# A branch unit behind each half-size product of v and g, the decays' parts between g's products, and three weight blocks multiplied beside x's loads

## The chip, the cores and the metric

The kernel runs on one core of one Trainium2 chip. The metric is the device time of one execution in microseconds. A core has a matrix engine (TensorE, PE in the rows), a vector engine (VectorE, DVE), a scalar engine (ScalarE, ACT), GpSimd (POOL) and SyncE (SP), which here only issues transfers. Each engine works through its own list of instructions in order and waits for the others through semaphores.

## The reference

A decoder trunk of one layer over 512 tokens and 1024 channels, in float32:

```python
h = rms_norm(x, norm_mix[l])
z = h @ w_in[l]
z_rnn, z_q, z_k, z_v, z_g, z_dec, z_mq, z_gate = jnp.split(z, split_idx, axis=-1)
xr = causal_dwconv(z_rnn, rnn_conv_w[l], rnn_conv_b[l])
out_a = rg_lru(xr, rg_w_a[l], rg_b_a[l], rg_w_x[l], rg_b_x[l], rg_lambda[l])
dec_logit = (z_dec @ gla_w_decay[l] + gla_b_decay[l]).astype(jnp.float32)
log_alpha = (jax.nn.log_sigmoid(dec_logit) / GLA_NORMALIZER).reshape(bsz, slen, GLA_HEADS, GLA_DK)
o_gla = chunked_gla(z_q, z_k, z_v, log_alpha)
out_b = rms_norm(o_gla, gla_norm[l]) * jax.nn.silu(z_g)
...
out_c = jnp.einsum("bhsm,bmhd->bshd", prob, mv).reshape(bsz, slen, MIX_WIDTH)
branches = jnp.stack([out_a, out_b, out_c], axis=2)
proj = jnp.einsum("bsnc,ncd->bsnd", branches, w_branch[l])
gates = jax.nn.sigmoid(z_gate).reshape(bsz, slen, N_BRANCHES, D_MODEL)
x = x + jnp.sum(gates * proj, axis=2) @ w_out[l]
```

After it come a gated MLP with a short causal convolution and a final norm, which the change leaves alone.

## The kernel before

**Products.** Each float32 operand is split in two rounded parts (`split`: ScalarE rounds the high part, L97, VectorE subtracts to get the low part, L98), and each product is three matmuls: high by high, high by low, low by high. `mm3` (L104) issues all but the start's.

**Units, steps and lead.** The program is a list (`prog`) of units and steps. A unit multiplies one weight block; its weights are fetched and split two units ahead (`AHEAD`). A gate or input unit (`hold`, `proj_in`) is 24 matmuls of 512 columns, a branch unit (`held`) 18, followed by VectorE's product with the gate (L641) and sum (L642). `weave` spreads steps among units by count; `blend` puts units of a second list among those of a first. Split weights live in three buffers each (`whi`, `wlo`), raw ones in four; SyncE issues the loads in the order in which the program asks for them.

**The start.** `start` multiplies two 1024 x 128 blocks of the input weights (raw query weights, `wch`) while x's eight row blocks still arrive; the products (L419) go two row blocks at a time. Further blocks follow as units (`qu`).

**Half-size products.** The products for v (`v_fast`, 400 columns with the low-rank decay columns) and g (`g_fast`, 384 columns) go by halves of tokens and channels in seven products instead of eight (`seven`): a1, a2, c1, c2, b1, b2, b3, each of two parts (p0, p1) of 12 matmuls. They share two banks of sums: after a1, a2, c1, ... the sum so far is read (`v_read`: L812 and L815 by ScalarE for a1 and a2, L821 and L824 by VectorE), and the next product is added to the same bank, so it has to wait for the read. c1, c2, b1 and b2 multiply sums of the normed activations (`h_sum1`, `h_sum4`, `h_quarter`), which VectorE adds and which are split like weights (`h_ready`). Some weights are sums too: GpSimd's transfers add a second block to one already loaded (L299).

**Around them.** `blend` puts four gate units (g0[0:4]) and three branch units (p0[0:3]) among the 28 parts of v and g. `lru_out` splits the recurrence's outputs (oa), which the branch units multiply. `decay_weights` loads the low-rank decay weights: a memset by GpSimd, three transfers by SyncE (L869), the rounding by ScalarE (L871) and VectorE (L873). `decay_in` transposes z_dec (L878, L880); `decay_logit` multiplies (L894) and takes Abs (L897) and the minimum with zero (L898); `decay_log` takes Exp (L904) and Ln (L907) of all four heads; `decay_sum` sums along the tokens; these ran beside the gate units g0[4:]. `decay_apply` (L928 to L939) with the branch units p0[3:], then `k_end` (transposes, L946), `intra`, `state`, `gla_out`, `gla_norm`, `gla_flip` and `silu` with the second branch's gate units g1, one list of steps for each.

## Time and profile before

| | before |
|---|---|
| median of 3 runs | 941.22 us (940.19 to 942.44) |
| the profiled execution | 941.12 us |
| its span, first to last instruction | 939.4 us |
| TensorE busy | 921.3 us, 98% |
| VectorE busy | 636.6 us, 68% |
| ScalarE busy | 488.2 us, 52% |

The profile is of one execution; the times in its rows count from the span's start. The instructions of TensorE overlap, so the length of one row (0.39 us for 512 columns) is not what it adds to the time: that is the distance from its start to the next one's.

### The profile page before, as it was taken

The numbers are of one execution on the slowest core, as the hardware profiler recorded it, in microseconds if no ns is written. First come the engines' busy times: TensorE is split into PE (matmuls) and PEld (weight loads), VectorE is DVE, ScalarE is ACT, GpSimd is POOL, SyncE is SP. The second block draws the span as 40 slices with busy tenths as digits, with TensorE's granted clock in tenths as the row PEclk, the third lists the DMA queues.
The fourth block names the chain that finished last, engine by engine and source line by source line (L and its number), as shares of the span: only waits on it lengthen the run. The fifth ranks groups of instructions, "written<-read, shape, count | busy, mean of one in ns | idle before, by whom it ended". The sixth has DMA issues, their size and how long they took to land.

```text
span 939.4 us, 11996 instructions
## 1 busy us (share of the span) xinstructions
PE 921.3 (98%) x4390; PEld 779.7 (83%) x4390; DVE 636.6 (68%) x1117; ACT 488.2 (52%) x796; POOL 90.9 (10%) x133
## 2 busy tenths in 40 slices
PE   9999999999998999999999999999999999999996
PEld 7899888888877998878888898888888888888885
DVE  6996745565788454795767665555686666698765
ACT  6765555685845345864434424344345444545544
POOL 0000000000053141000000000000010130012102
PEclk9999999999999999999999999999999999999999
DMA  7435223213369594231146401233364685357612
GB/s 250 160 119 196 88 80 108 85 59 106 111 161 186 130 202 135 76 119 51 51 135 225 167 23 45 92 111 112 135 114 138 146 227 119 110 126 184 162 45 89
DMA packets 45562, 116.93 MB, mean 124 GB/s; under 512 B 5520, under 2 KB 12864, under 8 KB 45504
## 3 DMA queue, kind: packets, MB, share of 16 engines
q1 hardware_dynamic: 33152, 94.28, 30.3%
q0 software_dynamic: 11776, 20.85, 13.0%
q10 hardware_dynamic: 576, 1.05, 0.3%
q8 instruction: 34, 0.56, 0.2%
q14 instruction: 24, 0.20, 0.1%
HBM read 111.69 MB, written 3.67 MB: 123 GB/s over the span
## 4 chain that ended last, share of the span: by engine, by line
PE 88%; DVE 6%; ACT 3%; issue 1%; DMA 1%; POOL 0%; SPq 0%; DVEq 0%; ACTq 0%
PE mm L104 81%; PE sm L104 2%; PE mm L419 1%; DVE wlo L98 1%; PE sm L983 1%; DMA m<-in_xT 1%; DVE f L920 0%; PE sm L969 0%; PE sm L604 0%; PE sm L985 0%; PE sm L585 0%; DVE f L774 0%; DMA f<-in_wdecay 0%; DVE r L98 0%; PE sm L956 0%
## 5 line engine op out<-in xcount | busy, mean ns | idle before, releaser
L98 DVE TENSOR_TENSOR wlo<-raw,whi 128x1024 fp32r<-128x1024 f32 (+2 forms) x155 | 172.4, 1115 | 161.0 <-PE mm L104 75.7
L97 ACT ACTIVATE whi<-raw 128x1024 fp32r<-128x1024 f32 (+2 forms) x155 | 149.7, 970 | 173.2 <-PE mm L104 159.5
L104 PE MATMUL mm<-whi,r 128*128 128x512 f32 (+2 forms) x568 | 172.7, 374 | 3.5 <-ACT r L97 1.8
L104 PE MATMUL mm<-h2l,whi 128*128 128x512 f32 x360 | 140.1, 389 | 0.0
L104 PE MATMUL mm<-h2h,whi 128*128 128x512 f32 x360 | 139.9, 389 | 0.0
L104 PEld LDWEIGHTS mm<-whi,r 128*128 128x128 f32 x568 | 106.4, 189 | 19.3 <-DVE r L98 2.3
L104 PE MATMUL mm<-hh,whi 128*128 128x512 f32 x288 | 113.8, 395 | 2.3 <-ACT whi L97 2.3
L104 PE MATMUL mm<-hl,whi 128*128 128x512 f32 x288 | 113.0, 392 | 0.0
L104 PE MATMUL mm<-wlo,r 128*128 128x512 f32 (+2 forms) x284 | 106.2, 374 | 0.4 <-DVE wlo L98 0.4
L104 PE MATMUL mm<-r,whi 128*128 128x512 f32 (+1 forms) x448 | 98.9, 369 | 0.0
L104 PEld LDWEIGHTS mm<-r,whi 128*128 128x128 f32 x448 | 77.8, 189 | 14.1 <-DVE r L98 0.2
L104 PE MATMUL mm<-h2h,wlo 128*128 128x512 f32 x360 | 88.9, 389 | 0.0
L97 ACT ACTIVATE whi<-f 128x512 fp32r<-128x512 f32 (+2 forms) x90 | 48.3, 581 | 74.6 <-PE mm L104 64.5
L104 PEld LDWEIGHTS mm<-h2h,wlo 128*128 128x128 f32 x360 | 67.6, 188 | 14.0
L104 PEld LDWEIGHTS mm<-h2l,whi 128*128 128x128 f32 x360 | 67.6, 188 | 14.0
L104 PEld LDWEIGHTS mm<-h2h,whi 128*128 128x128 f32 x360 | 67.5, 188 | 14.0
L98 DVE TENSOR_TENSOR wlo<-f,whi 128x512 fp32r<-128x512 f32 (+2 forms) x90 | 53.7, 631 | 35.8 <-ACT whi L97 19.6
L299 POOL DMA_DIRECT2D f<-in_wdown x40 | 35.1, 986 | 438.9 <-DVE wlo L98 415.8
L1127 DVE SCALAR_TENSOR_TENSOR f<-mm,prm,f 128x511 f32<-128x511 f32 x96 | 71.4, 745 | 6.9 <-ACT f L1125 6.1
L104 PE MATMUL mm<-hh,wlo 128*128 128x512 f32 x288 | 71.2, 389 | 0.0
L104 PEld LDWEIGHTS mm<-hh,whi 128*128 128x128 f32 x288 | 54.1, 188 | 13.9 <-ACT whi L97 3.0
L104 PEld LDWEIGHTS mm<-hh,wlo 128*128 128x128 f32 x288 | 54.1, 188 | 11.3
(243 smaller groups left out, 1313.2 us busy)
## 6 DMA issues: line engine op xcount, KB each, us to landing
raw<-in_wup SPq DMA_DIRECT2D x48, 512.0 KB, 3.6
raw<-in_wch SPq DMA_DIRECT2D x40, 512.0 KB, 3.6
f<-in_wdown POOLq DMA_DIRECT2D x40, 256.0 KB, 5.3
raw<-in_wbr SPq DMA_DIRECT2D x24, 384.0 KB, 3.1
raw<-in_wdown SPq DMA_DIRECT2D x14, 512.0 KB, 3.7
f<-in_wdown SPq DMA_DIRECT2D x20, 256.0 KB, 4.3
raw<-in_wout SPq DMA_DIRECT2D x8, 512.0 KB, 3.4
f<-in_wv POOLq DMA_DIRECT2D x16, 200.0 KB, 5.6
```

The lines of the kernel that those rows point to most:

```text
L97: nc.scalar.activation(hi, src, AF.Copy)
L98: (eng or nc.vector).tensor_tensor(out=lo, in0=src, in1=hi.bitcast(F32), op=ALU.subtract)
L104: nc.tensor.matmul(ps, lhsT=l, rhs=r, start=first and i == 0, stop=last and i == len(seq) - 1, skip_group_check=more)
L299: nc.gpsimd.dma_start(raw[to, p][j], src(q, p)[:, j, :], accum_op=ALU.add)
L419: nc.tensor.matmul(ps[u], lhsT=a, rhs=b, start=q == 0 and i in (0, 2), stop=q == KD - 2 and i >= len(seq) - 2)
L983: nc.tensor.matmul(ps[:, j, :], lhsT=sT[h][:, t, :], rhs=vt[t][hp][:, j, :], start=True, stop=t == 0)
L1127: nc.vector.scalar_tensor_tensor(out=a[:, j:], in0=ps[:, :S - j], scalar=col(C_FCW + 48 * (2 - j) + f), in1=a[:, j:], op0=ALU.mult, op1=AL ...
```

## The change

1. `start` multiplies three weight blocks instead of two, one row block of x at a time. The third block's split goes to ordinary slots instead of the `whi` and `wlo` buffers. SyncE's list gets the third block's four pieces in among x's.
2. `lru_rate`'s instructions are issued behind an `lru_split`, not in the start.
3. `run` replaces `blend`: it goes through lists written out by hand. In v_fast the order is a1, g0[0], g0[1], a2, c1, p0[0], g0[2], c2, b1, p0[1], b2, g0[3], b3, with `lru_out` in two groups; before, it was g0[0], a1, g0[1], a2, c1, c2, p0[0], b1, g0[2] and so on. Within the lists a scheduler may weave neighbours.
4. In g_fast come p0[2], `decay_in` and two `decay_logit`, g0[4], the other `decay_logit` and `decay_log`, p0[3], two `decay_sum`, g0[5], two `decay_sum`. g0[6] and g0[7] follow without them.
5. `decay_apply` goes with p0[4:] and g1[0:2], and the steps from `k_end` to the flips with g1[2:], six units instead of eight. g1[0] and g1[1] copy their sums first and take the sigmoid in place at the end (`late_gate`).
6. `h_sum1` is asked for eight units ahead instead of seven.

ScalarE in the value product, where the decay weights are rounded. Before (`mm_2571` and `mm_2578` are a1's banks, `mm_2556` that of g0[0]):

```order
L97 ACTIVATE whi_2616<-raw_2614 128x1024
L871 ACTIVATE r_2513<-f_2508 80x384
L1026 ACTIVATE f_2556<-mm_2531 128x512
L97 ACTIVATE whi_2636<-f_2278 128x400
L97 ACTIVATE whi_2636<-f_2279 128x400
L812 ACTIVATE f_2604<-mm_2571 128x400
L812 ACTIVATE f_2612<-mm_2578 128x400
L97 ACTIVATE r_2642<-f_2460 128x512
```

and now (`mm_2542` and `mm_2549` are a1's banks, `mm_2591` is g0[0]'s, `whi_2632` g0[1]'s weights, `whi_2655` c1's first):

```order
L97 ACTIVATE whi_2632<-raw_2630 128x1024
L97 ACTIVATE whi_2655<-f_2240 128x400
L97 ACTIVATE whi_2655<-f_2241 128x400
L889 ACTIVATE r_2529<-f_2524 80x384
L830 ACTIVATE f_2570<-mm_2542 128x400
L830 ACTIVATE f_2578<-mm_2549 128x400
L1044 ACTIVATE f_2616<-mm_2591 128x512
L97 ACTIVATE r_2618<-f_2177 128x512
```

The rounding of the decay weights stands in both ahead of the reads of a1's banks; before, g0[0]'s read and c1's weight split (which waits for g0[1]'s matmuls) stood between, now c1's weight split stands ahead of it and the reads follow at once.

SyncE's list around the decay weights. Before (`raw_2614` holds g0[1]'s weights, `raw_2646` and `raw_2696` c2's):

```order
L166 DMA raw_2614<-in_wch 128x1024
L303 DMA raw_2646<-in_wv 128x800
L303 DMA raw_2696<-in_wv 128x800
L869 DMA f_2508<-in_wdecay 16x384 x3
L166 DMA raw_2779<-in_wbr 128x768
L166 DMA raw_2922<-in_wch 128x1024
```

and now (`raw_2742` holds p0[0]'s weights, `raw_2748` c2's second part, `raw_2827` those of g0[2]):

```order
L303 DMA raw_2748<-in_wv 128x800
L166 DMA raw_2827<-in_wch 128x1024
L887 DMA f_2524<-in_wdecay 16x384 x3
L294 DMA f_2699<-in_wv 128x400
L294 DMA f_2700<-in_wv 128x400
```

The three transfers of the decay weights have moved behind the loads of p0[0] and g0[2].

ScalarE in g_fast, at the end of c2 and in b1. Now (`whi_3376` holds b1's second part in two halves, `whi_3400` p0[3]'s weights; L915 is Abs, L922 Exp, L925 Ln):

```order
L915 ACTIVATE f_3340<-sm_3338,prm 96x512
L97 ACTIVATE whi_3376<-f_2999 128x384
L915 ACTIVATE f_3346<-sm_3344,prm 96x512
L922 ACT_TABLE_LOAD
L922 ACTIVATE f_3340<-f_3340 96x512
L922 ACTIVATE f_3346<-f_3346 96x512
L925 ACT_TABLE_LOAD
L925 ACTIVATE f_3197<-f_3197 96x512
L925 ACTIVATE f_3203<-f_3203 96x512
L925 ACTIVATE f_3340<-f_3340 96x512
L925 ACTIVATE f_3346<-f_3346 96x512
L97 ACTIVATE whi_3376<-f_3000 128x384
```

Before, the Ln stood beside g0[4:], with only gate units' reads (L1026) and branch weights around:

```order
L1026 ACT_TABLE_LOAD
L1026 ACTIVATE f_3563<-mm_3538 128x512
L907 ACT_TABLE_LOAD
L907 ACTIVATE f_3477<-f_3477 96x512
L907 ACTIVATE f_3516<-f_3516 96x512
L907 ACTIVATE f_3522<-f_3522 96x512
L907 ACTIVATE f_3528<-f_3528 96x512
L1026 ACT_TABLE_LOAD
L1026 ACTIVATE f_3607<-mm_3582 128x512
L97 ACTIVATE whi_3620<-raw_3618 128x768
```

The Exp and Ln of all heads and their table loads now stand between the two halves of the weight split for b1's second part.

```diff
@@ -95,7 +95,7 @@
     def split(hi, lo, src, eng=None):
 
         nc.scalar.activation(hi, src, AF.Copy)
-        (eng or nc.vector).tensor_tensor(out=lo, in0=src, in1=hi.bitcast(F32), op=ALU.subtract)
+        return (eng or nc.vector).tensor_tensor(out=lo, in0=src, in1=hi.bitcast(F32), op=ALU.subtract)
 
     def mm3(ps, terms, first=True, last=True, more=False):
 
@@ -341,6 +341,15 @@
                            lambda key=key, p=p: run(key, p)))
         return us
 
+    def run(*parts):
+
+        for p in parts:
+            if isinstance(p, tuple):
+                unit(*p)
+            else:
+                for v in p:
+                    made_unit(*v) if isinstance(v, tuple) else step(v)
+
     def blend(us, fast, steps=()):
 
         for i, u in enumerate(us):
@@ -396,40 +405,45 @@
 
     def start():
 
-        raw = [wpool.tile([P, D], F32, tag="raw", name=nm("raw"), bufs=NRAW) for _ in range(2)]
-        whi, wlo = ([wpool.tile([P, D], F32R, tag=t, name=nm(t)) for _ in range(2)] for t in ("whi", "wlo"))
-        w = lambda a, u, k, n=1: a[u][:, k * P:(k + n) * P]
+
+        n = 3
+        raw = [wpool.tile([P, D], F32, tag="raw", name=nm("raw"), bufs=NRAW) for _ in range(n)]
+        whi, wlo = ([[wpool.tile([P, D], F32R, tag=t, name=nm(t))] for _ in range(2)] + [[rslot(), rslot()]]
+                    for t in ("whi", "wlo"))
+
+        def w(a, u, k, m=1):
+            j, k = divmod(k, KD // len(a[u]))
+            return a[u][j][:, k * P:(k + m) * P]
+
         for k in range(0, KD, 2):
             nc.sync.dma_start(xs["T"][k], xT[:, k, :])
-            for u in range(2):
-                nc.sync.dma_start(w(raw, u, k, 2), wch[u][:, k * P:(k + 2) * P])
+            for u in range(n):
+                nc.sync.dma_start(raw[u][:, k * P:(k + 2) * P], wch[u][:, k * P:(k + 2) * P])
             nc.sync.dma_start(xs["T"][k + 1], xT[:, k + 1, :])
             if k == 0:
                 nc.sync.dma_start(prm[:, KD:], par[:, KD:])
         for k in range(0, KD, 2):
             x_split([k])
-            for u in range(2):
-                split(w(whi, u, k, 2), w(wlo, u, k, 2), w(raw, u, k, 2))
+            for u in range(n):
+                split(w(whi, u, k, 2), w(wlo, u, k, 2), raw[u][:, k * P:(k + 2) * P])
             x_split([k + 1])
-        ps = [bank(), bank()]
-        for q in range(0, KD, 2):
-            seq = [(w(whi, u, k), xs["r"][k][j], u) for k in (q, q + 1) for u in range(2) for j in range(2)]
-            seq += [(w(wlo, u, k), xs["r"][k][0], u) for k in (q, q + 1) for u in range(2)]
-            for i, (a, b, u) in enumerate(seq):
-                nc.tensor.matmul(ps[u], lhsT=a, rhs=b, start=q == 0 and i in (0, 2),
-                                 stop=q == KD - 2 and i >= len(seq) - 2)
+        ps = [bank() for _ in range(n)]
+        for k in range(KD):
+            seq = [(whi, u, j) for j in range(2) for u in range(n)] + [(wlo, u, 0) for u in range(n)]
+            for i, (a, u, j) in enumerate(seq):
+                nc.tensor.matmul(ps[u], lhsT=w(a, u, k), rhs=xs["r"][k][j], start=k == 0 and i < n,
+                                 stop=k == KD - 1 and i >= len(seq) - n)
         x_squares(range(4))
         for p in ps:
             queries(p)
 
     step(start)
-    qu = [(wch[i], D, lambda w: queries(channel_major(w, KD, lambda k: xs["r"][k]))) for i in range(2, NM)]
+    qu = [(wch[i], D, lambda w: queries(channel_major(w, KD, lambda k: xs["r"][k]))) for i in range(3, NM)]
     xn = [lambda k=k: x_norm(k) for k in range(KD)]
-    weave(qu[:1], [])
     behind[0] = [lambda: x_squares(range(4, KD))]
-    weave(qu[1:2], [x_rstd])
-    weave(qu[2:3], [lambda: mem_load(1), x_bcast])
-    weave(qu[3:], xn[:2])
+    weave(qu[:1], [x_rstd])
+    weave(qu[1:2], [lambda: mem_load(1), x_bcast])
+    weave(qu[2:], xn[:2])
 
 
 
@@ -513,7 +527,7 @@
         return token_units(wmv[pr], 2 * DV, lambda k, t: tuple(mT[k][:, j, t * P:(t + 1) * P] for j in range(2)),
                            NMT, evac)
 
-    behind[2] = [lambda: mem_load(0)]
+    behind[1] = [lambda: mem_load(0)]
     vu = value_units(0) + value_units(1)
     step(mem_rstd)
     ku = [key_unit(i) for i in range(NM)]
@@ -650,6 +664,10 @@
     lsc, nsc = const.tile([P, NB], F32, name="lsc"), const.tile([P, NB], F32, name="nsc")
 
     def lru_rate():
+        with tc.issue_after(lru["split"].ins):
+            lru_rates()
+
+    def lru_rates():
 
         lam = prm[:, C_LAM:C_LAM + NB]
         lt, e, s1, q = stat(NB), stat(NB), stat(NB), stat(NB)
@@ -673,7 +691,7 @@
 
     def lru_split(b):
         lru["x", b] = (rslot((DK, S)), rslot((DK, S)))
-        split(*lru["x", b], xr[b])
+        lru["split"] = split(*lru["x", b], xr[b])
 
     def lru_weights(g):
         return wrg[g], 8 * DK, lambda w: lru.__setitem__(("w", g), w), 2
@@ -853,7 +871,7 @@
 
     def v_fast():
         pre = {k: [(2, lambda p, k=k: h_ready(k, p))] for k in ("c1", "c2", "b1", "b2")}
-        pre["c1"].append((7, h_sum1))
+        pre["c1"].append((8, h_sum1))
         pre["c2"].append((7, h_sum4))
         return seven(lambda q, p: wv[p, int(q[1]) - 1, int(q[2]) - 1], HP + LOW, 2, h_lhs,
                      pre, v_read, 4)
@@ -1020,31 +1038,37 @@
     step(decay_weights)
     gates = {}
 
-    def hold(n, d):
+    def hold(n, d, fn=AF.Sigmoid):
         def evac(ps):
             gates[n, d] = fslot()
-            nc.scalar.activation(gates[n, d], ps, AF.Sigmoid)
+            nc.scalar.activation(gates[n, d], ps, fn)
         return proj_in(18 + 8 * n + d, evac)
+
+    def late_gate(n, d):
+        nc.scalar.activation(gates[n, d], gates[n, d], AF.Sigmoid)
 
     def held(n, acts, d):
         return wbr[n, d], MIX, lambda w: branch(n, acts, d, gates.pop((n, d)))[1][2](w)
 
     g0, p0 = [hold(0, d) for d in range(KD)], [held(0, oa, d) for d in range(KD)]
-    g1 = [hold(1, d) for d in range(KD)]
-    tiles, heads = range(NT), range(H)
-    blend(g0[:2] + p0[:1] + g0[2:3] + p0[1:3] + g0[3:4], v_fast() + g_fast(), each(lru_out, range(NM)) + [lambda: None] * 15)
-
-    weave(g0[4:], [decay_in] + each(decay_logit, heads) + [decay_log] + each(decay_sum, heads))
-    weave(p0[3:], [qk_back] + each(decay_apply, heads))
-    for u, steps in zip(g1, (
-            each(k_end, tiles),
-            each(intra, heads) + [lambda t=t: silu(t, 0) for t in tiles],
-            [lambda n=n, hp=hp: state(n, hp) for n in range(2) for hp in range(2)],
-            [lambda t=t: silu(t, 1) for t in tiles] + [lambda hp=hp: state(2, hp) for hp in range(2)] +
-            [lambda t=t: gla_out(t, 0) for t in range(2)],
-            [lambda t=t: gla_out(t, 0) for t in range(2, 4)] + [lambda t=t: gla_out(t, 1) for t in range(2)],
-            [lambda: gla_norm(0)] + [lambda t=t: gla_out(t, 1) for t in range(2, 4)],
-            each(gla_flip, range(3)) + [lambda: gla_norm(1)],
+    g1 = [hold(1, d, AF.Copy if d < 2 else AF.Sigmoid) for d in range(KD)]
+    tiles, heads, vf, gf = range(NT), range(H), v_fast(), g_fast()
+
+    run(vf[:2], g0[0], each(lru_out, range(3)), vf[2:4], g0[1], each(lru_out, range(3, NM)), vf[4:6], p0[0],
+        vf[6:8], g0[2], vf[8:10], p0[1], vf[10:12], g0[3], vf[12:])
+    run(gf[:2], p0[2], [decay_in] + each(decay_logit, range(2)), gf[2:6], g0[4],
+        each(decay_logit, range(2, H)) + [decay_log], gf[6:10], p0[3], each(decay_sum, range(2)),
+        gf[10:12], g0[5], each(decay_sum, range(2, H)), gf[12:])
+
+    run(g0[6], g0[7], [qk_back])
+    weave(p0[4:] + g1[:2], each(decay_apply, heads))
+    for u, steps in zip(g1[2:], (
+            each(k_end, tiles) + each(intra, heads),
+            [lambda n=n, hp=hp: state(n, hp) for n in range(2) for hp in range(2)] +
+            [lambda t=t: silu(t, 0) for t in tiles],
+            [lambda hp=hp: state(2, hp) for hp in range(2)] + [lambda t=t: gla_out(t, 0) for t in tiles],
+            [lambda: gla_norm(0)] + [lambda t=t: silu(t, 1) for t in tiles] + [lambda t=t: gla_out(t, 1) for t in tiles],
+            each(gla_flip, range(3)) + [lambda: gla_norm(1)] + [lambda d=d: late_gate(1, d) for d in range(2)],
             each(gla_flip, range(3, 6)))):
         weave([u], steps)
     weave([held(1, ob, d) for d in range(KD)], [])
```

## Rows read from the trace of the kernel before

**Rows 1.** Busy time (share of the span) and instructions of an engine, from part 1 of the page.

```profile
PE 921.3 (98%) x4390; PEld 779.7 (83%) x4390; DVE 636.6 (68%) x1117; ACT 488.2 (52%) x796; POOL 90.9 (10%) x133
```

**Rows 2.** The chain of waits that ended last, part 4 of the page: shares by engine, then by engine and line (the row is long; its head is what counts).

```profile
PE 88%; DVE 6%; ACT 3%; issue 1%; DMA 1%; POOL 0%; SPq 0%; DVEq 0%; ACTq 0%
PE mm L104 81%; PE sm L104 2%; PE mm L419 1%; DVE wlo L98 1%; PE sm L983 1%; DMA m<-in_xT 1%; DVE f L920 0%; PE sm L969 0%; PE sm L604 0%; PE sm L985 0%; PE sm L585 0%; DVE f L774 0%; DMA f<-in_wdecay 0%; DVE r L98 0%; PE sm L956 0%
```

**Rows 3.** Two stretches of the start. Columns: from and to; length; busy us (and instructions) of TensorE, of its weight loads, of VectorE, ScalarE and GpSimd; granted clock; share of the DMA engines; GB/s.

```profile
5.00:13.40 8.40, 7.71 (x18) 4.93 (x18) 6.29 (x19) 6.11 (x15) 0.00 (x0) 1.00 0.91 302
13.40:20.90 7.50, 7.50 (x35) 6.16 (x34) 7.16 (x19) 5.00 (x10) 0.00 (x0) 1.00 0.82 303
```

**Rows 4.** The timeline of the start, TensorE and then ScalarE: start, length, engine, line, operation, out<-in, shape, how many, and in brackets the idle time before it and what ended it. `m` is x's transposed row block.

```profile
6.35 1.65 PE L419 MATMUL mm<-r,whi 128*128 128x512 f32 x3 [0.16 <-ACT whi L97]
8.47 2.07 PE L419 MATMUL mm<-r,whi 128*128 128x512 f32 x4 [0.47 <-ACT r L362]
...
5.88 0.42 ACT L97 ACTIVATE whi<-raw 128x256 fp32r<-128x256 f32 x1 [0.54 <-DMA raw<-in_wch]
7.70 0.72 ACT L362 ACTIVATE r<-m,prm 128x512 fp32r<-128x512 f32 x1 [1.40 <-DMA m<-in_xT]
```

**Rows 5.** The timeline of TensorE from the first gate unit (g0[0]) to g0[2], and after the first row the last of the 16 whi matmuls of that unit, the first of a1 and the 22nd of a1.

```profile
257.96 0.39 PE L104 MATMUL mm<-hh,whi 128*128 128x512 f32 x1
...
261.36 0.39 PE L104 MATMUL mm<-hl,whi 128*128 128x512 f32 x1
...
263.40 0.34 PE L104 MATMUL mm<-whi,hh 128*128 128x400 f32 x1
...
267.22 0.34 PE L104 MATMUL mm<-wlo,hh 128*128 128x400 f32 x1
...
269.07 0.50 PE L104 MATMUL mm<-hh,whi 128*128 128x512 f32 x1 [1.15 <-ACT whi L97]
...
281.32 0.81 PE L104 MATMUL mm<-whi,r 128*128 128x400 f32 x3 [0.75 <-DVE r L98]
...
285.04 0.45 PE L104 MATMUL mm<-whi,r 128*128 128x400 f32 x1 [1.78 <-ACT r L97]
...
286.99 1.37 PE L104 MATMUL mm<-whi,r 128*128 128x400 f32 x3 [0.95 <-DVE r L98]
...
304.26 0.50 PE L104 MATMUL mm<-hh,whi 128*128 128x512 f32 x1 [1.15 <-ACT whi L97]
```

**Rows 6.** Stretches of the value product; columns as in rows 3.

```profile
258.00:304.30 46.30, 40.16 (x190) 35.03 (x188) 40.55 (x70) 22.69 (x40) 20.45 (x29) 0.96 0.80 176
280.00:286.40 6.40, 3.39 (x15) 2.47 (x15) 6.40 (x17) 4.85 (x9) 6.34 (x8) 1.00 0.90 129
286.40:290.00 3.60, 3.01 (x9) 2.99 (x10) 2.22 (x4) 0.11 (x1) 0.00 (x0) 0.53 1.02 211
```

**Rows 7.** The timeline of ScalarE in the value product, and the split of a 768-column weight tile from a later place. L871 rounds the decay weights, L1026 reads a gate unit's bank, L812 (two instructions) the two banks of a1.

```profile
267.96 1.06 ACT L97 ACTIVATE whi<-raw 128x1024 fp32r<-128x1024 f32 x1 [1.31 <-PE mm L104]
271.25 0.53 ACT L871 ACTIVATE r<-f 80x384 fp32r<-80x384 f32 x1 [2.23 <-DMA f<-in_wdecay]
271.68 0.58 ACT L1026 ACTIVATE f<-mm 128x512 f32<-128x512 f32 x1
...
273.95 0.88 ACT L812 ACTIVATE f<-mm 128x400 f32<-128x400 f32 x2
...
279.64 0.62 ACT L97 ACTIVATE r<-f 128x512 fp32r<-128x512 f32 x1
...
318.77 0.85 ACT L97 ACTIVATE whi<-raw 128x768 fp32r<-128x768 f32 x1 [1.24 <-PE mm L104]
```

**Rows 8.** The decay weights' transfers by their source line: duration of an issue, first and last start; then the time from issue to landing.

```profile
L869 SPq DMA_DIRECT2D f<-in_wdecay x3: 326/411/412, 266.6 to 267.5; - x3
...
DMA to landing us min/median/max: 2.6/3.7/3.8
```

**Rows 9.** The low half of a 1024-column weight tile on VectorE, in the timeline of VectorE.

```profile
269.05 1.23 DVE L98 TENSOR_TENSOR wlo<-raw,whi 128x1024 fp32r<-128x1024 f32 x1 [0.55 <-ACT whi L97]
```

**Rows 10.** The timeline of ScalarE beside g0[4:]: L897 is Abs, L904 Exp, L907 Ln, L1026 a gate unit's sigmoid.

```profile
370.13 0.69 ACT L897 ACTIVATE f<-sm,prm 96x512 f32<-96x512 f32 x1 [1.48 <-PE sm L894]
370.83 1.28 ACT L904 ACT_TABLE_LOAD   x1
...
379.13 0.67 ACT L897 ACTIVATE f<-sm,prm 96x512 f32<-96x512 f32 x1
379.70 1.15 ACT L904 ACTIVATE f<-f 96x512 f32<-96x512 f32 x2
...
382.76 1.28 ACT L907 ACT_TABLE_LOAD   x1
384.06 2.20 ACT L907 ACTIVATE f<-f 96x512 f32<-96x512 f32 x4
```

**Rows 11.** k_end's first transposes in the timeline of TensorE, and the multiplication that they wait for in that of VectorE.

```profile
415.47 0.47 PE L946 MATMUL sm<-ident,f 96*128 96x96 f32 x3 [1.64 <-DVE f L934]
...
414.74 0.68 DVE L934 TENSOR_TENSOR f<-f,f 96x512 f32<-96x512 f32 x1
```

**Rows 12.** Stretches of decay_apply and of what follows it until the flips; columns as in rows 3.

```profile
390.00:420.00 30.00, 28.36 (x137) 23.26 (x136) 29.57 (x47) 19.66 (x29) 1.99 (x4) 1.00 0.32 108
420.00:464.00 44.00, 44.00 (x232) 38.56 (x231) 28.22 (x74) 19.99 (x53) 0.00 (x0) 1.00 0.18 56
```

## The prediction

> **What bounds the kernel now.** The page's busy times come first: TensorE works through 98% of the span, VectorE 68%, ScalarE 52% [rows 1]. The chain that ended last says the same, 88% of it TensorE [rows 2]. The change keeps every product (the matmuls have the same shapes and the same number), so TensorE's work is a floor, and what can be won is the time in which TensorE stands or runs slowly. I looked for it first in the start, then in TensorE's waits by time, and read the other engines only around those places. Four places matter.
>
> *The start.* From 5.0 to 13.4 us TensorE was given 18 matmuls of 512 columns, from 13.4 to 20.9 us 35 [rows 3]: about 0.43 us each against 0.21 (0.227 in the steady stretch, below). The granted-clock column reads 1.00 for both, so the pace, not that column, tells the slow stretch. Two waits lie in it, 0.16 us for the second weight block's high part and 0.47 us for x's second row block, whose split began when its transfer landed at 7.70 [rows 4].
>
> *The stretch of the value product* (v_fast with the first gates and branch units). A 512-column matmul takes (261.36 − 257.96)/15 = 0.227 us, a 400-column one (267.22 − 263.40)/21 = 0.182 us [rows 5]. Between 257.96 and 304.26 stand two gate units (48 × 0.227 = 10.9), one branch unit (18 × 0.227 = 4.1), four pairs of the seven products (96 × 0.182 = 17.5), one more pair (4.4) and two transposes (0.4): 37.2 us of work in 46.3 us. 9.1 us are lost: 1.15 us each at 269.07 and 304.26, where a gate unit waits for ScalarE's weight split into a buffer that the matmuls just before it had held; waits of 0.75, 1.78 and 0.95 us at 281.32, 285.04 and 286.99, where c1's and c2's activations are late [rows 5], because VectorE was busy for all of 280.0 to 286.4 [rows 6]; and the stretch from 286.4 to 290.0, where the granted clock was 0.53 [rows 6], near the lower of its two levels (1.2 of 2.4 GHz), after these waits.
>
> *k_end* waits 1.64 us for VectorE at 415.47, because decay_apply's last multiplications for head 3 start only at 414.74 [rows 11]; VectorE was busy 29.57 of 30 us there [rows 12].
>
> *The rest* runs without a wait worth counting.
>
> **The change, part by part.**
>
> *Three blocks in the start: −1.5 us.* Nine matmuls now follow each row block of x instead of six, so x's transfers are waited for less; 4 × 128 KB more are fetched in the start, 0.52 MB at 302 GB/s [rows 3] = 1.7 us, which the third block's own load had to move anyway. At the slow pace the first nine matmuls take 9 × 0.43 = 3.8 us, from 5.4 to 9.3, and x's second block is then there (8.47 before [rows 4], plus one more piece of 128 KB, 0.43 us), so the 0.47 us wait goes. Bound one: the fast pace begins at 13.4 as before. Then 18 of the 72 matmuls are done and 54 × 0.227 = 12.3 us follow, to 25.7; before, the 48 matmuls and the third block's 24 ended at 20.9 + 24 × 0.227 = 26.3. Gain 0.6. Bound two: the fast pace comes earlier by the 4 us in which TensorE now works without a gap; each us saves 1 − 0.21/0.43 = 0.5 us, so the gain is 0.6 + 2 = 2.6. I take the middle, 1.5. lru_rate's 18 short VectorE instructions go to a stretch where VectorE is not full: nothing.
>
> *The order of the value stretch: −3.9 us.* The order is now a1, g0[0], g0[1], a2, then c1, p0[0], c2 and g0[2] woven. What goes: both 1.15 us waits, because the buffer that g0[1] splits into was freed by a1, one whole unit (5.4 us) earlier, against 1.06 us for a split [rows 7]. What comes: the decay weights. Their three transfers were issued at 266.6 to 267.5 and landed 3.7 us later [rows 8]; only then could ScalarE round them (L871, 271.25 [rows 7]). In SyncE's order they now stand behind a weight load that waits for g0[1]'s low half. That split runs when g0[0] is done: 257.96 + 4.4 + 5.4 = 267.8, plus 1.23 us on VectorE [rows 9] = 269.1. The load itself and three issues of 0.41 us [rows 8] follow, the last starts at 270.4, landing 274.1. On ScalarE the rounding (0.5) stands ahead of the two reads of a1's banks (0.44 each [rows 7]), and a2, which adds to these banks, must wait for them: it starts at 275.1 instead of 273.2 (267.8 + 5.4). **New wait 1.9 us**; before, those reads had 3 us to spare. Next, p0[0]'s weight split (0.85) now stands ahead of c1's activation split (0.62 [rows 7]) on ScalarE and can start only when a2 is done: c1 waits about 1.5 us. Then VectorE, which waited for the decay weights too and still has 40.55 us of work in these 46.3 [rows 6] (four more splits come in, two go), is late for four low halves in c1 and p0[0]; by counting its list at 0.60 us an instruction I get 0.4, 0.5, 0.8 and 0.15, so 1.85. New waits 1.9 + 1.5 + 1.85 = 5.2, against 9.1 lost before: gain 3.9. Bounds: none of the new waits occurs and 9.1 are won; or the clock falls again as in 286.4 to 290.0 and the waits after it double: nothing is won.
>
> The Trainium skill ("TensorE: Matmul & The Clock Gate", table of its opening section) says that ScalarE and VectorE take their instructions strictly in order. This speaks against the change, and the rows agree: L1026's read of g0[0] at 271.68 follows straight behind L871, which had waited 2.23 us for its transfer [rows 7].
>
> *The decays' parts between g_fast's products: +3.1 us.* Before, decay_in to decay_sum ran beside g0[4:], without a wait of TensorE. Now ScalarE has, between the two halves of the weight split for b1's second part: an Abs (0.57, from 379.13 to 379.70), a table load (1.28), two Exp (1.15), a second load (1.28) and four Ln (2.20) [rows 10]. Counting from the start of g0[4]: TensorE needs 5.4 (unit) + 0.5 (two decay products) + 40 matmuls of 384 columns at 0.175 (0.182 × 384/400) = 12.9 us until it wants the second half. ScalarE's first half waits for the buffer that c2's first part frees at 8.0; after it 8.0 + 0.5 + 0.57 + 1.28 + 1.15 + 1.28 + 2.20 + 0.5 = 15.5. **New wait 2.6 us**, and p0[3]'s weight split behind it (0.85) comes 0.5 us after TensorE has done the two matmuls that stand ahead: 3.1. Bounds 0 (if the buffer's release lets the first half go earlier) and 4. The same four Ln beside g0[4:] cost nothing before, so nothing is won back there.
>
> The Trainium skill ("ScalarE: Activation LUTs", What ACT_TABLE_LOAD costs) puts a switch at 1.28 us of load and 1.38 us of drain. By that, the two loads here would cost 2.8 us more and this term would be 5.9. The trace disagrees: the load at 370.83 starts 0.01 us after the Abs of 370.13 has ended, and the load at 382.76 is followed by the first Ln at 384.06, 0.02 us after its end [rows 10], so no drain is seen.
>
> *decay_apply and k_end: −1.5 us.* decay_apply now runs beside four branch units and two gate units, (4 × 18 + 2 × 24) × 0.227 = 27.3 us, and k_end comes two gate units later, so the 1.64 us wait goes. The rest (k_end to the flips) has six gate units instead of eight: VectorE's 28.22 us of 44 [rows 12] less two weight splits (2.4) in 33 us and the small matmuls. That fits; one place is tight, the last gla_out, whose bank is read behind the first norm's chain: 0.2. The four added table loads of this part fall where ScalarE has 10 us in 30 free [rows 12]: nothing.
>
> **Sum.** −1.5 − 3.9 + 3.1 − 1.5 = −3.8 us. The profiled execution took 941.12 us with a span of 939.4; the median of the runs is 941.22, so I go from there: **937.4 us**.
>
> **Rivals.**
> 1. *All waits vanish.* The decay weights land in time or the order on ScalarE leaves slack: −1.5 − 9.1 − 1.5 and 0 to 1 for the decays, about 930 us. For it: all four places have a wait by name. Against it: both of the queues that I counted are in order.
> 2. *The gains are given back.* The half clock returns after a2's or the decays' wait (286.4 to 290.0 shows it after 3.5 us of waits within 6 us [rows 5, 6]) at some 2 us, and the start gives 0.6: −3.8 + 2 + 0.9, about 940.3, no measurable change. By the drain of the Trainium skill's ScalarE page ("ScalarE: Activation LUTs") the sum would come to 941.2 − 3.8 + 2.8 = 940.2.
> 3. *Slower: one late transfer holds two queues.* ScalarE and VectorE both have an instruction on the decay weights' transfer in front of everything that c1 and p0[0] need. If it lands 2 us later than I put it (its 3.7 us is a median under 0.8 DMA load [rows 6, 8]), every wait of that stretch grows by it: 1.9 + 2, 1.5 + 2, 1.85 + 2, with the half clock's 2: 13.2 lost instead of 9.1, and −1.5 + 4.1 + 3.1 − 1.5 = +4.2 in all, 945 us. It decides from about 11 us lost in the stretch on. Against it: VectorE's backlog cannot grow by more than the delay once.
> 4. *The order doesn't matter*: TensorE's waits only move, 941.
>
> **Chances.** Forecast 0.48, rival 1 0.17, rival 2 with 4 0.22, rival 3 0.13. 0.2% is 1.9 us, about what a measurement of this kernel can tell from no change. The forecast's own range is 935 to 940, of which a tenth is within 0.2%. Faster 0.48 × 0.9 + 0.17 = 0.60, same 0.05 + 0.20 = 0.25, slower 0.13 + 0.02 = 0.15. The range goes from 931, most of rival 1's, to 942.5.
>
> **What would show it.** Start: the 72 matmuls end at 24 to 25.7. Value stretch: no wait of g0[1] or g0[2]; a2 waits about 1.9 us for ScalarE's read of a bank behind the decay weights' rounding; c1 waits for its activation's split. g_fast: b1's second part waits 2 to 3 us for a weight split behind four Ln. k_end without a wait. I am wrong if a2 starts at once, if the Ln row ends before TensorE comes to b1, or if a stretch at the lower clock stands where there was none.

## The result, and the profile after

| | before | after |
|---|---|---|
| median (20 runs each, side by side) | 939.30 us (936.78 to 942.44) | 942.30 us (940.74 to 944.52) |
| ratio | | 1.0034, 95% interval 1.0025 to 1.0042 |
| profiled execution / its span | 941.12 / 939.4 us | 942.34 / 940.5 us |

The change makes the kernel 3.0 us slower. The forecast was 937.4 us, with 942.5 as the upper end. It was reckoned from 941.22, the median of three executions of the kernel before; the median of the twenty is 939.30. So the forecast was 3.8 us less, and 3.0 us more were measured. Of the executions in the section below, one, of the run "Ln later", took 1548.85 us at a mean granted clock of 0.557 and is left out of that run's ratio.

TensorE's waits in the profile after (line of the waiting matmul, engine and line waited for; us in total, times, longest). L830 reads a1's and a2's banks, L495 is VectorE's read of a key bank:

```profile
PE mm L104 <- ACT f L830: 3.1, 1, 3.1
PE mm L104 <- ACT whi L97: 2.7, 1, 2.7
PE mm L104 <- ACT r L97: 1.6, 2, 1.5
...
PE mm L104 <- DVE r L98: 0.8, 2, 0.6
PE mm L104 <- DVE f L495: 0.6, 1, 0.6
PE mm L104 <- DVE wlo L98: 0.6, 1, 0.6
```

The 1.15 us waits for g0[1]'s and g0[2]'s weight splits and the 1.64 us of k_end are gone [rows 5, 11]. Two new ones stand at the top, of 3.1 and 2.7 us. The timeline of TensorE has them (start, length, ..., in brackets the idle time and what ended it):

```profile
274.42 0.45 PE L104 MATMUL mm<-whi,hh 128*128 128x400 f32 x1 [3.12 <-ACT f L830]
...
282.06 0.45 PE L104 MATMUL mm<-whi,r 128*128 128x400 f32 x1 [1.45 <-ACT r L97]
...
290.48 1.10 PE L104 MATMUL mm<-r,whi 128*128 128x512 f32 x3 [0.61 <-DVE r L98]
...
358.71 0.61 PE L104 MATMUL mm<-whi,r 128*128 128x384 f32 x2 [2.71 <-ACT whi L97]
...
360.76 0.69 PE L104 MATMUL mm<-wlo,r 128*128 128x384 f32 x1 [0.58 <-DVE wlo L98]
```

The first row is a2, the second c1, the third the branch unit p0[0], the last two b1's second part of g. Behind both long waits the granted clock was at its lower level (windows; columns as in rows 3, the clock stands third from the end):

```profile
5.00:13.40 8.40, 8.12 (x35) 6.17 (x35) 6.80 (x14) 6.79 (x17) 0.00 (x0) 1.00 1.01 350
13.40:20.90 7.50, 7.50 (x35) 6.22 (x34) 6.42 (x10) 5.57 (x11) 0.00 (x0) 1.00 0.85 313
274.50:278.40 3.90, 3.90 (x13) 3.87 (x14) 3.89 (x8) 1.84 (x5) 0.00 (x0) 0.57 0.63 92
...
360.40:363.80 3.40, 3.04 (x9) 2.85 (x10) 3.29 (x7) 0.71 (x2) 1.31 (x2) 0.50 0.27 41
```

The first of these waits is followed by 0.50 from 275.0 on, the second from 360.4 to 363.8. In the start, TensorE now does 35 matmuls in the window in which it did 18 [rows 3], and the 72 of the three blocks end at 22.4 us.

To see where the time lies, I took the distance from each matmul's start to the next, less the median distance of its shape in the same trace, and summed this over stretches. What comes out is the time lost to waits and to slow matmuls together, in us (good to some 0.3 us in a stretch, since a median that is 1 ns off counts once for every matmul of its shape):

| stretch of the span | 0–20 | 20–120 | 260–320 | 340–380 | 400–420 | 420–460 | whole |
|---|---|---|---|---|---|---|---|
| before | 6.9 | 1.3 | 8.6 | 0.2 | 2.1 | 0.4 | 20.4 |
| after | 3.0 | 3.0 | 8.7 | 5.7 | 0.0 | 1.1 | 22.5 |

The value stretch (260–320) won nothing in these two executions, the decays between g's products (340–380) cost 5.5, k_end's wait is gone, and the start's gain of 3.9 is followed by a loss of 1.7. The profiled execution of before was 1.8 us above the median of its runs (941.12 against 939.30), that of after was at its median; so the two profiles alone show less than the 3.0 us, and the first question is whether the start's 3.9 belong to the kernel or to the execution.

### The profile page after: what moved, and what is told of

Read it like the earlier page. It is cut to its first block, busy times and chain, and to the rows that moved or that the text cites. A ratio compares the mean times of both kernels' runs of the same rounds, so it can differ in the third digit from the quotient of the medians.

```text
span 940.5 us, 12015 instructions
## 1 busy us (share of the span) xinstructions
PE 920.6 (98%) x4390; PEld 779.5 (83%) x4390; DVE 637.3 (68%) x1120; ACT 493.6 (52%) x805; POOL 91.2 (10%) x133
## 4 chain that ended last, share of the span: by engine, by line
PE 92%; DVE 3%; ACT 2%; issue 1%; DMA 1%; POOL 0%; SPq 0%; DVEq 0%; ACTq 0%
PE mm L104 85%; PE mm L434 2%; PE sm L104 2%; DVE wlo L98 1%; DMA f<-in_wdecay 0%; PE sm L987 0%; DMA raw<-in_wch 0%; PE sm L974 0%; PE sm L1001 0%; ACT whi L97 0%; PE sm L618 0%; PE sm L599 0%; PE sm L1134 0%; DVE r L98 0%; DVE m L391 0%
## 5 line engine op out<-in xcount | busy, mean ns | idle before, releaser
L98 DVE TENSOR_TENSOR wlo<-raw,whi 128x1024 fp32r<-128x1024 f32 (+3 forms) x154 | 170.3, 1111 | 152.9 <-PE mm L104 72.6
L97 ACT ACTIVATE whi<-raw 128x1024 fp32r<-128x1024 f32 (+3 forms) x154 | 148.7, 970 | 177.2 <-PE mm L104 153.6
L104 PE MATMUL mm<-r,whi 128*128 128x512 f32 (+1 forms) x432 | 96.3, 370 | 1.7 <-DVE r L98 0.8
L104 PEld LDWEIGHTS mm<-r,whi 128*128 128x128 f32 x432 | 75.3, 190 | 16.3 <-DVE r L98 1.7
```

The source lines that it names most:

```text
L97: nc.scalar.activation(hi, src, AF.Copy)
L98: return (eng or nc.vector).tensor_tensor(out=lo, in0=src, in1=hi.bitcast(F32), op=ALU.subtract)
L104: nc.tensor.matmul(ps, lhsT=l, rhs=r, start=first and i == 0, stop=last and i == len(seq) - 1, skip_group_check=more)
```

## The experiments

The theories, in pairs. On the start: A, its gain is as large as the profiles show; B, it is a matter of the one execution that was profiled. On a2's wait: C, the transfer of the decay weights ahead of the reads of a1's banks causes it and the slow stretch behind it; D, the engines' own work would hold a2 there too. On b1's wait: E, Exp, Ln and their table loads ahead of the weight split cause it; F, g's weights come late by themselves. Each run was timed beside the kernel before, with 4 to 12 executions of its own; the median of the kernel before was 939.65 to 939.79 us there. Gains against the changed kernel ("after") are differences of the two ratios to the kernel before.

**The start alone.** Before, with the three-block start and its lists, without the move of lru_rate:

```diff
-        raw = [... for _ in range(2)]
+        n = 3
+        raw = [... for _ in range(n)]
...
-    behind[2] = [lambda: mem_load(0)]
+    behind[1] = [lambda: mem_load(0)]
```

> The kernel before with the three-block start alone. Theory A (the start really gives what the two profiles show, 26.3 to 22.4 us at the end of the third block, and the loss lies elsewhere): 939.3 - 3.9 = 935.4 us. Rival B (the slow first 8 us of the profile before were the chance of that one execution, since 20 runs of the kernel before spread over 5.7 us): within 1 us of the kernel before, 938.5 to 939.5.

Measured: 938.87 us, ratio 0.9995 (0.9984 to 1.0006). This is what theory B forecast.

**The changed kernel with the old start.**

> The changed kernel with the two-block start of before. Theory A: the start's gain is lost, 942.3 + 3.9 = 946.2 us. Rival B: no change by it, 942 to 943. In both the waits at a2 and in b1 of g stay (3.1 and 2.7 us).

Measured: 941.78 us, ratio 1.0029 (1.0017 to 1.0040), against 1.0034 with the new start. Theory B's number again. This edit leaves `lru_rate` behind the `lru_split`, where the change had put it. The profiles of all kernels with either start say why. The time lost in the first 20 us was 6.9, 4.6, 5.4, 4.7 and 4.5 us in the five with the old start (the kernel before had the largest loss), and 3.0, 3.2, 5.0 and four times 3.3 in the seven with the new one: 5.2 against 3.5 in the mean, a gain of 1.7. From 20 to 120 us it was 1.2 to 1.3 with the old start and 3.0 to 3.1 with the new one: 1.8 given back. The largest piece of that is this wait, in the profile after:

```profile
57.30 1.93 PE L104 MATMUL mm<-r,whi 128*128 128x256 f32 x14 [0.63 <-DVE f L495]
```

The key units need banks that VectorE reads (L495) behind x's and the memory's norms; as I read it, the 24 matmuls drawn into the start are one unit less to cover these norms. That the old start doesn't have the loss is shown, this reason for it is not.

**Only the decay weights' transfers earlier.** The changed kernel; the memset and the three transfers are asked for some 50 us earlier, the rounding stays in its place:

```diff
+    step(lambda: decay_loads())
     weave(b2[8:12], [s for p in zip(each(lru_scan, lo), each(lru_gates, hi)) for s in p])
...
-    def decay_weights():
-        wy = fslot((KZ, H, DK))
+    def decay_loads():
+        wy = gla["wy0"] = fslot((KZ, H, DK))
         nc.gpsimd.memset(wy, 0.0)
         for c in range(0, KZ, 2 * LOW):
             nc.sync.dma_start(wy[c:c + LOW], wdecay)
+    def decay_weights():
+        wy = gla.pop("wy0")
         r = gla["wy"] = rslot((KZ, H, DK))
```

> The changed kernel with only the decay weights' memset and three transfers put earlier (in the recurrence's branch units); their rounding stays where it was. In the run before this one the rounding had been moved too, and VectorE's list with it. Theory C (the transfer in front of the reads of a1's banks is the whole of a2's wait): a2 has no wait, the stretch at 0.50 behind it is gone or stands elsewhere, and 942.3 - 3.1 - 1.7 = 937.5 us. Rival D (the engines' work is the bound there): the 3.1 us come back as waits for VectorE in c1 and p0[0], 941.5 to 942.5 us.

Measured: 936.69 us, ratio 0.9976 (0.9966 to 0.9987), 5.4 us better than after. This is theory C. The time lost in 260–320 fell from 8.7 to 2.3. These are the only waits of TensorE left there, and the granted clock was at its upper level throughout:

```profile
278.24 1.36 PE L104 MATMUL mm<-whi,r 128*128 128x400 f32 x6 [0.39 <-DVE r L98]
...
284.52 1.10 PE L104 MATMUL mm<-r,whi 128*128 128x512 f32 x3 [0.61 <-DVE r L98]
```

What the wait was made of, in the profile after: ScalarE's rounding (L889) and the bank reads (L830), SyncE's issues, and the transfers' landing; then the landing with the early loads:

```profile
273.46 0.52 ACT L889 ACTIVATE r<-f 80x384 fp32r<-80x384 f32 x1 [2.97 <-DMA f<-in_wdecay]
273.89 0.87 ACT L830 ACTIVATE f<-mm 128x400 f32<-128x400 f32 x2
...
265.12 0.33 SPq L166 DMA_DIRECT2D raw<-in_wbr  x1
266.03 0.33 SPq L303 DMA_DIRECT2D raw<-in_wv  x1
267.20 0.33 SPq L166 DMA_DIRECT2D raw<-in_wch  x1
267.62 1.58 SPq L887 DMA_DIRECT2D f<-in_wdecay  x3
...
DMA to landing us min/median/max: 4.7/5.1/5.3
```

```profile
L888 SPq DMA_DIRECT2D f<-in_wdecay x3: 382/412/413, 215.5 to 216.4; - x3
...
DMA to landing us min/median/max: 2.7/3.0/3.2
```

The three small transfers took 5.1 us from issue to landing, behind loads of 384, 400 and 512 KB issued within 2.1 us; 50 us earlier, behind a single load of 512 KB, they took 3.0. That the other loads are what held them was not tried apart. Had they landed in 3.7 us as before [rows 8], a2's wait would be some 1.7 us (an estimate: 3.12 less 1.4).

**The whole decay-weights step earlier,** rounding included, ahead of `lru_decay(1)`.

> The changed kernel with the decay weights loaded and rounded before the last branch units of the recurrence instead of in the value product; nothing else asked for. Theory C (a2 waits because ScalarE stands at the decay weights' transfer, and the clock's lower level follows from that wait): a2's wait of 3.1 us goes, with it the stretch at 0.50 after 275.0 (some 1.7 us): 942.3 - 4.8 = 937.5 us. Rival D (VectorE's and ScalarE's work in the value product is the bound, the transfer only the place where it shows): c1 and p0[0] then wait longer by about what a2 waited, 941.5 to 942.5 us.

Measured: 941.32 us, ratio 1.0021 (1.0010 to 1.0033). Not a clean test. a2's wait went, but the rounding now stood ahead of the recurrence's Exp and Tanh on ScalarE, VectorE's last scan of the recurrence began at 268.2 instead of 263.0, and g0[1]'s low weight half came late:

```profile
268.28 2.67 PE L104 MATMUL mm<-hh,wlo 128*128 128x512 f32 x8 [2.00 <-DVE wlo L98]
```

The granted clock was at 0.50 from 269.6 to 273.0. Some 2 of the 5.2 us by which the scan is later belong to the profiled execution, not to the edit: at 944.00 us it was the longest of the twelve, and its start lost 5.0 us instead of 3.0. Moving the transfers alone was worth 5.4 us; with the rounding moved too, 1.2 are left, which the two intervals hardly tell from nothing.

**The early transfers in the kernel before.** The same edit, old order.

> The kernel before with one edit: the memset and the three transfers of the decay weights are asked for some 50 us earlier, the rounding stays where it was. It asks what the new order of the value stretch adds. Theory G (the order is worth its gain once the transfer is early): in the old order the two waits of 1.15 us for a weight split and c1's and c2's late activations are there all the same, only ScalarE's 2.23 us wait for the transfer goes; the time stays within 2 us of before, 938 to 940 us. Theory H (the transfer was the cause in the old order too: VectorE, busy through 280 to 286.4, had lost its lead in waiting for it): the waits of 0.75, 1.78 and 0.95 us and the stretch at the lower clock at 286.4 go with it, 3.5 + 1.8 = 5.3 us, 934.5 us, as much as the early loads gave the changed kernel, and the new order adds nothing to it.

Measured: 938.05 us, ratio 0.9984 (0.9973 to 0.9996). Nearer to G. The old order keeps its waits:

```profile
266.62 0.50 PE L104 MATMUL mm<-hh,whi 128*128 128x512 f32 x1 [1.15 <-ACT whi L97]
...
280.61 0.45 PE L104 MATMUL mm<-whi,r 128*128 128x400 f32 x1 [1.35 <-ACT r L97]
...
282.81 0.82 PE L104 MATMUL mm<-whi,r 128*128 128x400 f32 x3 [0.85 <-DVE r L98]
...
285.15 0.74 PE L104 MATMUL mm<-r,whi 128*128 128x512 f32 x2 [0.98 <-ACT whi L97]
...
299.62 0.50 PE L104 MATMUL mm<-hh,whi 128*128 128x512 f32 x1 [1.15 <-ACT whi L97]
```

They add up to 5.5 us, where before had 5.8 [rows 5]. What went in this profile is the stretch at the lower clock [rows 6]: 6.7 us lost instead of 8.6. The clock stood at 1.00 where the kernel before had 0.53:

```profile
286.40:290.00 3.60, 3.60 (x22) 3.60 (x21) 1.56 (x4) 0.96 (x2) 0.40 (x1) 1.00 1.10 291
```

This execution took 936.40 us, near the shortest of its twelve. Eight of them, at a mean granted clock of 0.997 or 0.998, took 936.3 to 938.7 us; the four at 0.993 to 0.996 took 939.7 to 940.6, so the stretch was probably not gone from those four (they were not profiled). In these profiles the new order alone wins nothing (8.7), the early transfers alone 1.9 (1.5 by the ratio of the runs), and both together 6.3 (8.6 to 2.3).

**Ln later.** The changed kernel with `decay_log` behind p0[3] and the sums behind it:

```diff
-        each(decay_logit, range(2, H)) + [decay_log], gf[6:10], p0[3], each(decay_sum, range(2)),
-        gf[10:12], g0[5], each(decay_sum, range(2, H)), gf[12:])
+        each(decay_logit, range(2, H)), gf[6:10], p0[3], [decay_log], gf[10:12], each(decay_sum, range(2)), g0[5],
+        gf[12:], each(decay_sum, range(2, H)))
```

> The changed kernel with decay_log asked for behind p0[3] and the decay_sum steps behind b2, so that ScalarE splits the second half of b1's weights and p0[3]'s weights ahead of the Ln and its table load. The gate units stay between g's products. Theory E (ScalarE's order is what costs): b1's wait of 2.7 us, 1.0 us behind it and the stretch at 0.50 go: 942.3 - 5.4 = 936.9 us. Rival F (g's weights come late by themselves): a wait of 1 us or more stays at b1 or moves to the next unit, 939.5 to 940.5 us.

Measured: 935.82 us, ratio 0.9966 (0.9952 to 0.9979). This is theory E: the loss in 340–380 fell from 5.7 to 0.3. ScalarE in the profile after, then with this edit (L922 Exp, L925 Ln):

```profile
351.61 0.67 ACT L915 ACTIVATE f<-sm,prm 96x512 f32<-96x512 f32 x1
352.30 1.28 ACT L922 ACT_TABLE_LOAD   x1
353.59 1.15 ACT L922 ACTIVATE f<-f 96x512 f32<-96x512 f32 x2
354.76 1.28 ACT L925 ACT_TABLE_LOAD   x1
356.06 2.19 ACT L925 ACTIVATE f<-f 96x512 f32<-96x512 f32 x4
358.15 0.51 ACT L97 ACTIVATE whi<-f 128x384 fp32r<-128x384 f32 x1
```

```profile
351.78 0.67 ACT L915 ACTIVATE f<-sm,prm 96x512 f32<-96x512 f32 x1
352.35 0.51 ACT L97 ACTIVATE whi<-f 128x384 fp32r<-128x384 f32 x1
352.88 1.28 ACT L922 ACT_TABLE_LOAD   x1
354.17 0.63 ACT L922 ACTIVATE f<-f 96x512 f32<-96x512 f32 x1
354.71 0.83 ACT L97 ACTIVATE whi<-raw 128x768 fp32r<-128x768 f32 x1
```

b1's second weight half (358.15 and 352.35) starts 6.5 us after the Abs in the one and 0.6 us after it in the other. TensorE had no wait in that stretch. The edit moves `decay_sum` as well as `decay_log`, so it tests the two together.

**The decays back beside g0[4:].** The changed kernel, with only p0[2] and p0[3] among g's products.

> The changed kernel with decay_in to decay_sum woven with g0[4:] again, as before, and g's products beside p0[2] and p0[3] alone. Theory E (the Exp, Ln and table loads in front of b1's second weight half cost the 2.7 us wait, 1.0 us of waits behind it and a stretch at the clock's lower level, 1.7 us): 942.3 - 5.4 = 936.9 us. Rival F (g_fast without gate units among its products is itself tight, since its weights come by added transfers): new waits of about 3 us there, 940 us.

Measured: 940.36 us, ratio 1.0015 (1.0001 to 1.0029). Better by 1.8 us and no more: b1 now waits for a weight split of which ScalarE says that its transfer was late:

```profile
351.07 0.44 PE L104 MATMUL mm<-whi,r 128*128 128x384 f32 x1 [1.19 <-ACT whi L97]
...
350.50 0.52 ACT L97 ACTIVATE whi<-f 128x384 fp32r<-128x384 f32 x1 [1.70 <-DMA f<-in_wg]
```

In this arrangement F holds: 3.4 us are lost in 340–380. As I read it, g's products come faster than their weights without gate units among them; the late transfer is shown, its reason is not.

**The last part alone.** Before, with decay_apply beside p0[3:] and g1[:2], k_end one unit pair later, and the late gates.

> The kernel before with the last part of the change alone: decay_apply beside p0[3:] and g1[0:2], the steps from k_end on beside six gate units, two gates copied and made late. If that part does what the prediction said (k_end's wait of 1.64 us goes, little comes): 939.4 - 1.5 = 937.9 us. Rival: six gate units are too few and the added table loads show, 939.5 us or more.

Measured: 939.61 us, ratio 1.0005 (0.9994 to 1.0017). k_end's wait for VectorE turned into one for ScalarE's copy of its bank, with a lower clock behind it:

```profile
425.55 0.55 PE L946 MATMUL sm<-ident,f 96*128 96x96 f32 x4 [1.55 <-ACT f L948]
...
426.80:430.30 3.50, 3.50 (x19) 3.50 (x18) 2.47 (x3) 0.78 (x1) 0.00 (x0) 0.51 0.09 11
```

The profile lost 1.3 us in 400–460 instead of 2.5, but the runs show no gain, or one of 0.6 us at most. This is not quite the changed kernel's list (p0[3] and the shift from g's products are missing), where no such wait stands.

**Both repairs,** early transfers and later Ln, with the new start:

> Both of the above together. If the two waits and the clock stretches behind them are independent, the gains add: with theories C and E 942.3 - 4.8 - 5.4 = 932.1 us; with D and F 939 to 940 us.

Measured: 930.78 us, ratio 0.9913 (0.9899 to 0.9926). The gains add up within their intervals: 5.4 and 6.4 us singly, 11.4 together. TensorE is busy for 43.9 of 45 and 40 of 40 us where both repairs lie:

```profile
260.00:305.00 45.00, 43.90 (x209) 37.73 (x208) 38.96 (x65) 23.87 (x42) 16.84 (x24) 1.00 0.81 193
340.00:380.00 40.00, 40.00 (x200) 35.84 (x199) 27.77 (x42) 29.17 (x41) 7.62 (x12) 1.00 0.61 172
```

**Both repairs with the old start:**

> The version with both repairs (decay loads early, Ln later), but with the start as it was in the kernel before: two weight blocks beside x's loads, lru_rate in the start. If the new start is worth nothing in the median, as the start alone said (ratio 0.9995), the time is that of both repairs, 930 to 932 us, 0.990 to 0.992 of before. If the start is worth the 1.5 us of the prediction once the later waits are gone, it is 932.3 or more (0.9925 or more); if it is worth the 3.9 us by which the profiled starts differ, 934.5. If the new start costs more downstream (waits at 33, 57 and 105 us) than it gives, it is below 930.

Measured: 930.67 us, ratio 0.9902 (0.9888 to 0.9916). The start is worth nothing here either. The text above says that `lru_rate` was in the start; the edit left it behind the `lru_split`, as in the changed kernel. These two are the fastest kernels of the study, 9 us below before.

## Why the prediction was wrong

The places, the engines and the order of the new waits were right, but for one small wait. The sum failed in what a wait costs: in the value stretch it set waits and slow matmuls of before (9.1 us) against the bare waits of after (5.2). The last of its own signs of being wrong, a stretch at the lower clock where there was none, appeared twice.

- **Start, −1.5 forecast, 0 measured** (−1.5 to +0.6 by the interval of the start alone; +0.5 and +1.0 by the two kernels that were run with either start). Inside the start the size holds (−1.7 in the mean of the profiles), but by luck, since its working does not: the slow pace lasts for a time that changes from execution to execution, which bound one took as fixed, and in the profile after the 72 matmuls ended at 22.4, ahead of both bounds. The step that failed is a term put at nothing without a reason: what the new start costs behind it was not asked, and between 20 and 120 us 1.8 are given back. That x's and the memory's norms lose one unit of cover is my reading of it, not shown.
- **Value stretch, −3.9 forecast, 0 measured in the two profiles (−0.7 in the means below).** The old waits went. The new ones were put at 1.9, 1.5 and 1.85, and are 3.12, 1.45 and 0.95: 5.2 forecast, 5.5 measured. a2's is larger because the transfer took 5.1 us to land instead of the 3.7 of before [rows 8]. The large error is on the other side. The 9.1 us lost before are 5.8 of waits [rows 5] and 3.3 of slow matmuls and short gaps, among them those of the stretch at 0.53 [rows 6]. This gross sum I set against the new waits alone. The new waits of 5.5 us bring 3.2 of slow matmuls as well, 8.7 in all. Set like against like, the forecast's own waits give 5.8 less 5.2, a gain of 0.6 and not of 3.9. Rivals 2 and 3 had 2 us for a half clock; the forecast had none. Rival 3's late transfer came in part, 1.4 of its 2 us, and of the waits only a2's grew.
- **Decays between g's products, +3.1 forecast, +5.5 measured.** The first wait is right (2.6 forecast, 2.71 measured, for the Ln and the table loads as told). The second has the size (0.5 and 0.58) but not the cause: it was forecast for p0[3]'s weight split on ScalarE, and is b1's low half on VectorE, behind two scans (L938) of decay_sum (the two rows under this list). What the waits bring was left out: 3.4 us at half clock, where every second us is lost (1.7), and slow matmuls beside it (0.5). This is rival 2's mechanism; rival 2 allowed 2 us for the half clock once, after a2's or the decays' wait, and it came after both.
- **decay_apply and k_end, −1.5 forecast, −1.4 measured** (−2.1 and +0.7). Alone, in the run above, it gave nothing; in the changed kernel it was not undone, so its −1.4 rests on profiles alone.
- **The table loads.** The Trainium skill's drain of 1.38 us ("ScalarE: Activation LUTs", What ACT_TABLE_LOAD costs) is not seen after either: the loads at 352.30 and 354.76 are followed by the first Exp and Ln 1.29 and 1.30 us later. By the Trainium skill's figure b1's wait would be 2.8 us longer (an estimate). The forecast had left the drain out, and rightly.

```profile
357.93 2.33 DVE L938 TENSOR_TENSOR_SCAN f<-chm,f 96x512 f32<-96x512 f32 x2
360.18 0.53 DVE L98 TENSOR_TENSOR wlo<-f,whi 128x384 fp32r<-128x384 f32 x1
```

The sum of the two profiles, with the start at 0, is then 0 + 0.1 + 5.5 − 1.4 = 4.2 us, where 3.0 were measured. The difference lies in the executions: before's own slow stretch varies. In the start alone and the last part alone, whose value stretch is that of before, the granted clock was low for 6.9 us against 3.6 [rows 6]; here is the row of the start alone:

```profile
283.40:290.30 6.90, 6.07 (x18) 6.01 (x19) 4.58 (x8) 1.71 (x3) 0.17 (x1) 0.51 1.07 236
```

Means over the profiles that share a stretch bring the sum to what was measured. The value stretch lost 8.6, 9.2 and 9.1 us in the old order, and 8.7, 8.1, 8.0 and 8.4 in the four with the new order and the late transfers: −0.7. The decays (340–380) lost 5.7, 5.4, 5.8 and 5.4 where they stand between g's products as in the change, against 0.2: +5.4. The last part (400–460) lost 1.0 in the same four against 2.5 in the kernels with the old one: −1.5. The start and what follows it to 120 us lost 6.56 with the new start against 6.44 with the old: +0.1. Together they give +3.3 us.

## What to carry to other kernels

When a wait of TensorE is weighed against another, count both the same way: the wait, and the slow matmuls behind it where the clock falls, which it did behind both long new waits here. A small transfer whose reader stands ahead of a bank read in an in-order engine should be asked for long before, and long activation chains with table switches should not stand between the two halves of a weight split. Units drawn ahead in the program may be units that no longer cover what comes after them: the start won 1.7 us here and 1.8 were lost behind it, though this reason for it was not shown. One profile does not price a start whose pace changes from execution to execution.

## What the runs showed of the hardware

- A wait's price depends on whether the clock falls behind it: a2's 3.12 us was followed by 0.50 from 275.0 to 278.4, b1's 2.71 by 0.50 from 360.4 to 363.8, k_end's 1.55 in the last part alone by 0.51 from 426.8; k_end's 1.64 in the kernel before [rows 11] and b1's 1.19 with the decays back by none. All nine waits of 2.0 us or more in the twelve profiles had such a fall, within 1.7 us of the wait's end (once it began while TensorE still waited). With the transfers early in the old order, five waits of 5.5 us in all within some 34 us had none in the profile. I had looked for a fall after several waits close together, not after one.
- TensorE's pace in the start rises at a point that changes from one profiled execution to the next (between 4.7 and 13.4 us in the twelve profiles), whichever the start is. It is worth some 2 us: with the old start, 6.9 us were lost in the first 20 where the pace rose last, 4.5 to 4.7 where it rose early. The kernel before's profile, on which the start's estimate rested, was the latest of them.
- Three transfers of 16x384 took 3.0 us to land behind one weight load of 512 KB and 5.1 us behind three of 1.3 MB in all; that the loads are the cause was not tried apart.
